# Turned activations moved 4, 8, 16 or 48 bytes inside their tiles, in a one-core kernel of three transformer blocks

## The chip, the cores and the metric

The kernel runs on one core of one Trainium2 chip. The metric is the device time of one execution, in microseconds (us), as the median of several runs; lower is better. One execution was also profiled, and the rows below come from it.

## What is computed

The reference runs three layers on 256 tokens of width 1024, batch 1, everything in float32. The parts that matter here are the large products, activation times weight:

```python
for i in range(DEPTH):                      # two layers
    ...
    h = h + jnp.concatenate([mix, mem_out], axis=-1) @ w_out
    z = rms_norm(h, norm_ffn[i])
    if i % 2 == 0:
        h = h + swiglu(z, ffn_w_gate[j], ffn_w_up[j], ffn_w_down[j])      # width 2816
    else:
        h = h + moe_swiglu(z, moe_router[j], moe_w_gate[j], moe_w_up[j], moe_w_down[j])
...
# third layer (second_block): two kinds of attention, then
f = jnp.square(jax.nn.relu(h @ w_ff1[layer])) @ w_ff2[layer]              # width 4096
```

`moe_swiglu` sends each token to 2 of 8 experts, each a SwiGLU network of inner width 3584. Its weights are 352 MB of the roughly 500 MB that the kernel reads.

## The kernel before

**The products.** Every large product is made of three TensorE passes, so that float32 accuracy is kept with a faster operand type (`float32r`). An activation x is split into a high part and a low part, and so is a weight w; `mm3` (L393) adds xh·wh, xl·wh and xh·wl into one PSUM bank. The first operand of `PE.matmul` is the stationary one: a block of the activation, 128 rows by 128 tokens, that is loaded into the array (LDWEIGHTS in the profile, row PEld). The second operand, the weight, streams past it, mostly 512 columns at a time (MATMUL, row PE). Each of the three passes loads its own stationary block, so there is one load per matmul. `gemm_col` (L398) does products with a weight's columns, `gemm_row` (L428) those of the down projections, both through `mm3` at L394 to L396.

**Turned activations.** The stationary block needs the contraction along the partitions, so activations are turned: TensorE transposes them (L387), and `split` (L374) writes the high part with ScalarE (L375) and the low part with VectorE (L376). The tiles that hold them are
- `xth`, `xtl`: 8 chunks of 256 tokens, made by `new_xt` (L491) for the inputs of the dense products: the attention and convolution projections, both feed-forward networks, the output projections;
- `hth`, `htl` in `ffn` (L919): 4 chunks of 256 tokens, the inner activations of the two dense feed-forward networks;
- `xeh`, `xel` in `gather` (L1446): 8 chunks of 128 tokens, the tokens that one expert was given (L375 and L376 again write them, behind a product with a one-hot matrix at L1453);
- `hth`, `htl` in the expert loop (L1577): 4 chunks of 128 tokens, the inner activations of an expert.

In one place the roles are exchanged: in the convolution's input projection (L1156 to L1158) the weight is stationary and `xth` or `xtl` streams, 256 columns at a time.

**Where the tiles lie.** A partition of SBUF is a row of bytes. The pools are so padded that, in the built program, the left-hand pools begin at multiples of 128 bytes and those on the right-hand side 64 bytes behind one. All the four kinds of turned tile lie at a multiple of 128 bytes, but for the three `new_xt(1)` pairs on the right (the input of the first feed-forward network, `z0`, and the two layers' memory tokens), which lie 64 behind. The chunks inside a tile are 512 or 1024 bytes apart, so each 128-token block begins where its tile does, as far as the place within 128 bytes goes. The weights' high and low parts (`whi`, `wlo`) sit in rings of slots: the five main pairs of slots at multiples of 128, and extra pairs on the right-hand side, used in the mixers and the third layer, 64 behind.

**The weight stream.** `Stream` (L52 on) loads 1 MB pieces of weights in the order of use (SP queue, L93) into a ring of raw slots, ScalarE copies a unit of 128x1024 to its high part (L107), VectorE subtracts to get the low part (L122), and TensorE uses both. A raw slot is loaded again once L122 has read it, a `whi`/`wlo` slot is filled again once TensorE has used it.

**The expert loop** runs over 8 experts and 7 blocks of 512 inner columns each, 56 blocks. One block is 24 passes for the gate, 24 for the up product (stationary `xeh`, `xel`) and 24 for the down product of the block before (stationary `hth`, `htl`), 72 passes of 512 columns in all.

Of the kernel before, what the change touches and what calls it, by code (L numbers as in the profile page):

```python
# [11 lines left out]
F32R = mybir.dt.float32r  # L12
# [11 lines left out]
T = 256  # L24
# [139 lines left out]
def two_blocks(tc, A, out):  # L164
# [14 lines left out]
    def bank(i, shape=(128, 512)):  # L179
        return psp.tile(list(shape), F32, name=f"b{i}", tag=f"b{i}", bufs=1)  # L180
# [26 lines left out]
    def ffn_blocks(width):  # L207
        b = blocks(width)
        return b[-1:] + b[:-1] if b[-1][1] < 512 else b
# [46 lines left out]
    def pool(es, name, bufs, side=None):  # L256
        return es.enter_context(tc.tile_pool(name=name, bufs=bufs, side=side, reuse_waits="tile"))
# [116 lines left out]
    def split(src, hi_, lo_):  # L374
        S.activation(hi_, src, AF.Copy)  # L375
        V.tensor_tensor(lo_, src, hi_.bitcast(F32), op=OP.subtract)  # L376

    def turn(*a):
        run(turns(*a))
# [18 lines left out]
    def gemm_col(o, xt, n, tbs=(0, 1), outer=False):  # L398

        th, tl = xt  # L400
        nu = 8 // (4 if n == 256 else 2)
        na = 8 // nu

        def one(u, i, tb):
            wh, wl = u
            for kk in range(na):
                k = i * na + kk
                mm3(o[tb], th[:, k, tb * 128:tb * 128 + 128], tl[:, k, tb * 128:tb * 128 + 128],
                    wh[:, kk, :], wl[:, kk, :], k == 0, k == 7)

        if outer:
            us = W.take(nu)
            for tb in tbs:
                for i, u in enumerate(us):
                    one(u, i, tb)
                    if tb == tbs[-1]:
                        W.done(1)
                    yield
        else:
            for i in range(nu):  # L420
                u = W.take(1)[0]
                for tb in tbs:
                    one(u, i, tb)
                    if tb == tbs[-1]:
                        W.done(1)
                    yield
# [38 lines left out]
    def run(g):  # L465
        for _ in g:
            pass

    class Bg:
# [12 lines left out]
        def finish(self):  # L482
            while self.g is not None:
                self.pump()
# [3 lines left out]
    xq = ExitStack()  # L488
    xtp = [pool(lv, "xtp", 1), pool(xq, "xtq", 1, "right")]

    def new_xt(i=0):  # L491
        return (xtp[i].tile([128, 8, T], F32R, name="xth"), xtp[i].tile([128, 8, T], F32R, name="xtl"))

    def norm_only(src, grow, xn=None, upd=None, dve=False):
        if xn is None:
# [409 lines left out]
    def ffn(xt, width, gated, t1, finish, tick=lambda: None, free=lambda b: None, near_end=lambda: None):  # L905


        with ExitStack() as es:
            fp = pool(es, "ffn", 2)
            acc = [[bank(4), bank(5)], [bank(6), bank(7)]]  # L910
            prev = None
            rot = 0
            bl = ffn_blocks(width)

            def ticked(g):
                for _ in g:
                    tick()

            def turned(hn, n, rot):  # L919
                ht = (fp.tile([128, 4, T], F32R, name="hth"), fp.tile([128, 4, T], F32R, name="htl"))  # L920
                for tb in range(2):
                    turn(hn[tb], n // 128, ht[0], ht[1], 0, tb, [rot + tb])
                return ht

            late = None
            for fi, (c0, n) in enumerate(bl):
                gv = [bank(rot)[:, 0:n], bank(rot + 1)[:, 0:n]]
                r2 = (rot + 2) % 4
                ub = 6 if fi == 0 else r2
                uv = [bank(ub)[:, 0:n], bank(ub + 1)[:, 0:n]]  # L930
                g = gemm_col(gv, xt, n, outer=fi == 0)
                ug = gemm_col(uv, xt, n, outer=fi == 0) if gated else ()
                if fi == 0:

                    first = [x for x in (g, ug) if x for i in range(8 // (4 if n == 256 else 2))]
                    for i, x in enumerate(first):
                        if i == len(first) - (1 if gated else 1):
                            t1()
                        next(x)
                    W.hold = False  # L940
                    W.most = 1
                if late is not None:

                    for _ in range(4):
                        next(g)
                        tick()
                    prev = (turned(*late), late[1], True)
                    late = None
                    W.most = 99
                ticked(g)  # L950
                hn = [fp.tile([128, 512], F32, name=f"sg{tb}") for tb in range(2)]
                for tb in range(2):
                    S.activation(hn[tb][:, 0:n], gv[tb], AF.Silu if gated else AF.Relu)
                ticked(ug)
                for tb in range(2):
                    V.tensor_tensor(hn[tb][:, 0:n], (uv if gated else gv)[tb], hn[tb][:, 0:n], op=OP.mult)
                free(rot)
                if prev is not None:
                    ticked(gemm_row(acc, prev[0], list(range(prev[1] // 128)), prev[2], False))
                if fi == 0:  # L960
                    late = (hn, n, rot)
                else:
                    prev = (turned(hn, n, rot), n, False)
                rot = r2
            near_end()
            g = gemm_row(acc, prev[0], list(range(prev[1] // 128)), False, True, outer=True)
            for i in range(prev[1] // 128):
                next(g)
            finish(acc, 0)
            run(g)  # L970
            finish(acc, 1)
# [200 lines left out]
    for c in range(6):  # L1172
# [6 lines left out]
        def tick():  # L1179
            dg.pump(3)  # L1180
            dt.pump(3)
            heads.pump(1)
# [249 lines left out]
    mp = pool(mo, "moe", 2)  # L1432
# [12 lines left out]

    def gather(p):  # L1446

        xe = (mp.tile([128, 8, 128], F32R, name="xeh", bufs=1), mp.tile([128, 8, 128], F32R, name="xel", bufs=1))
        for g in range(2):
            b = bank(6 + g)  # L1450
            for j in range(4):
                for tb in range(2):
                    PE.matmul(b[:, j * 128:j * 128 + 128], zN[:, tb, (g * 4 + j) * 128:(g * 4 + j) * 128 + 128],  # L1453
                              p[:, tb], start=tb == 0, stop=tb == 1)
            split(b.rearrange("p (j t) -> p j t", t=128), xe[0][:, g * 4:g * 4 + 4],
                  xe[1][:, g * 4:g * 4 + 4])
        return xe
# [88 lines left out]
    for e in range(NE):  # L1546
        xe = xes.pop(e)
        for fi, (c0, n) in enumerate(bl):
            rot = 2 * ((e * len(bl) + fi) % 2)
            gb, ub = bank(rot), bank(rot + 1)  # L1550
            run(gemm_col([gb], xe, n, tbs=(0,)))
            sg = growp.tile([128, D], F32, name="grow")[:, 0:512]
            S.activation(sg, gb, AF.Silu)
            if last is not None:
                combine(*last, 1)
                last = None
            run(gemm_col([ub], xe, n, tbs=(0,)))
            V.tensor_tensor(sg, ub, sg, op=OP.mult)
            if fi == len(bl) - 1 and e + 1 < NE:
                xes[e + 1] = gather(hot[e + 1])  # L1560
            if prev is not None:
                pe_, pacc, pht, pfi = prev
                run(gemm_row([pacc], pht, list(range(4)), pfi == 0, pfi == len(bl) - 1, tbs=(0,)))
                if pfi == len(bl) - 1:
                    last = (pe_, rows_of(pacc), scatter(hot.pop(pe_)))
            if e == 0 and fi == 1:
                gates()
                mci = counts()
                gcol = const.tile([128, 16], F32, name="gcol")
                for i, nm in enumerate(("mixg", "ffng")):  # L1570
                    V.scalar_tensor_tensor(gcol[:, 8 * i:8 * i + 8], colsA[:, 8 + 24 * i:16 + 24 * i], 1.0,
                                           P[:, R[nm]:R[nm] + 8], op0=OP.add, op1=OP.mult)
            if fi == 4 and e + 1 < NE:
                hot[e + 1] = chosen(e + 1, 0)
            if fi == 0:
                acc = [bank(4), bank(5)]
            ht = tuple(mp.tile([128, 4, 128], F32R, name=f"ht{x}", bufs=1) for x in "hl")  # L1577
            turn(sg, 4, ht[0], ht[1], 0, 0, [rot])
            prev = (e, acc, ht, fi)
            if last is not None:  # L1580
                combine(*last, 0)
# [161 lines left out]
    for g in range(2):  # L1743
        Z, A1 = [], []
        for i in range(4):
# [8 lines left out]
            t = sp_.tile([128, 384], F32, name="ab")  # L1754
# [255 lines left out]
```

## Time and profile before

| what | value |
|---|---|
| median of 3 runs | 1871.54 us (1871.01 to 1878.94) |
| the profiled execution | 1873.42 us |
| its span, first to last instruction | 1871.0 us |
| TensorE busy | 1822.2 us, 97% of the span |
| VectorE busy | 1455.6 us, 78% |
| ScalarE busy | 1227.1 us, 66% |
| weight loads (PEld) busy | 1497.7 us, 80% |
| mean rate of the DMA | 269 GB/s |

The page divides the span in 40 slices; TensorE is at nine tenths or more in all but three of them. A matmul's duration in the profile contains the time in which its last columns run through the array, and successive matmuls overlap. What a pass really costs is the distance from its start to the start of the next one, which is called its pitch below.

### The profile page before, as it was taken

Reading aid. Unit: us, or ns where it says so; the run is one execution under the profiler, and the core shown is the slowest. Engines: PE = TensorE matmul, PEld = TensorE weight load, DVE = VectorE, ACT = ScalarE, POOL = GpSimd, SP = SyncE. Lnnn points to the kernel's source line nnn. Section 1 sums busy time; section 2 is a strip of 40 time slices with the busy share of each in tenths; the row PEclk is TensorE's granted clock in tenths of the full one; section 3 lists DMA queues with packets and bytes.
Section 4 is the critical chain, followed back from the end, with each engine's and each line's share of the span. In section 5 each row is a group of like instructions: output and inputs, shape, how many; then the busy total and the mean of one; then the engine's idle time right before and its main releaser. Section 6 shows DMA issues by size and latency. Waiting matters only on the chain. (4 is left out here: it accounts for less than half of the span.)

```text
span 1871.0 us, 23916 instructions
## 1 busy us (share of the span) xinstructions
PE 1822.2 (97%) x8782; PEld 1497.7 (80%) x8782; DVE 1455.6 (78%) x1743; ACT 1227.1 (66%) x1605; POOL 39.3 (2%) x63
## 2 busy tenths in 40 slices
PE   7999999999999999999999999999999989999998
PEld 6787888898778888788788888887888867678886
DVE  5556988688799899898998998888988864467553
ACT  5645444465588777787787787877877775546442
POOL 1100000000000000000000000000000010010000
PEclk9999999999999999999999999999999999999999
DMA  7325997562699999899999998999999644237540
GB/s 275 134 80 193 397 334 287 196 190 75 230 338 378 341 342 383 321 369 347 343 374 350 338 375 316 366 355 339 368 357 335 248 144 151 75 104 265 183 158 23
DMA packets 224933, 503.95 MB, mean 269 GB/s; under 512 B 8308, under 2 KB 25896, under 8 KB 224808
## 3 DMA queue, kind: packets, MB, share of 16 engines
q1 hardware_dynamic: 223688, 499.37, 74.4%
q0 software_dynamic: 832, 2.46, 0.5%
q8 instruction: 70, 1.15, 0.2%
q10 hardware_dynamic: 288, 0.52, 0.1%
q14 instruction: 55, 0.45, 0.1%
HBM read 501.26 MB, written 1.06 MB: 268 GB/s over the span
## 5 line engine op out<-in xcount | busy, mean ns | idle before, releaser
L122 DVE TENSOR_TENSOR wlo<-wraw,whi 128x1024 fp32r<-128x1024 f32 (+1 forms) x894 | 1053.2, 1219 | 182.5 <-ACT whi L107 171.6
L107 ACT ACTIVATE whi<-wraw 128x1024 fp32r<-128x1024 f32 (+1 forms) x894 | 928.4, 1057 | 265.1 <-PE b L395 238.3
L394 PE MATMUL b<-whi,xeh 128*128 128x512 f32 x896 | 359.2, 401 | 0.0
L396 PE MATMUL b<-wlo,xeh 128*128 128x512 f32 x896 | 349.8, 390 | 0.0
L395 PE MATMUL b<-whi,xel 128*128 128x512 f32 x896 | 349.0, 389 | 0.0
L394 PE MATMUL b<-whi,xth 128*128 128x512 f32 (+2 forms) x656 | 257.1, 392 | 6.3 <-ACT xth L375 2.3
L394 PE MATMUL b<-whi,hth 128*128 128x512 f32 x664 | 261.9, 394 | 0.8 <-PEq L1503 0.6
L395 PE MATMUL b<-whi,htl 128*128 128x512 f32 x664 | 260.9, 393 | 0.4 <-DVE htl L376 0.2
L396 PE MATMUL b<-wlo,hth 128*128 128x512 f32 x664 | 260.7, 393 | 0.0
L395 PE MATMUL b<-whi,xtl 128*128 128x512 f32 (+2 forms) x656 | 251.6, 384 | 1.7 <-DVE xtl L376 0.9
L396 PE MATMUL b<-wlo,xth 128*128 128x512 f32 (+2 forms) x656 | 251.7, 384 | 1.2 <-DVE wlo L122 1.2
L395 PEld LDWEIGHTS b<-whi,xel 128*128 128x128 f32 x896 | 168.4, 188 | 37.0 <-issue 3.3
L394 PEld LDWEIGHTS b<-whi,xeh 128*128 128x128 f32 x896 | 168.3, 188 | 36.3 <-issue 3.3
L396 PEld LDWEIGHTS b<-wlo,xeh 128*128 128x128 f32 x896 | 168.1, 188 | 36.0
L394 PEld LDWEIGHTS b<-whi,xth 128*128 128x128 f32 x656 | 125.3, 191 | 33.0 <-ACT xth L375 4.2
L394 PEld LDWEIGHTS b<-whi,hth 128*128 128x128 f32 x664 | 125.8, 189 | 27.8 <-ACT hth L375 1.3
L395 PEld LDWEIGHTS b<-whi,htl 128*128 128x128 f32 x664 | 125.7, 189 | 27.4 <-DVE htl L376 1.0
L396 PEld LDWEIGHTS b<-wlo,hth 128*128 128x128 f32 x664 | 125.7, 189 | 26.9
L396 PEld LDWEIGHTS b<-wlo,xth 128*128 128x128 f32 x656 | 125.1, 191 | 26.2 <-DVE wlo L122 2.5
L395 PEld LDWEIGHTS b<-whi,xtl 128*128 128x128 f32 x656 | 125.3, 191 | 25.8 <-DVE xtl L376 2.7
L375 ACT ACTIVATE hth<-b 128x512 fp32r<-128x512 f32 (+1 forms) x84 | 48.3, 593 | 87.5 <-PE b L387 87.5
L376 DVE TENSOR_TENSOR htl<-b,hth 128x512 fp32r<-128x512 f32 (+1 forms) x84 | 56.2, 683 | 48.7 <-ACT hth L375 48.7
(348 smaller groups left out, 1438.4 us busy)
## 6 DMA issues: line engine op xcount, KB each, us to landing
wraw<-in_moe_w_gate_dram SPq DMA_DIRECT2D x112, 1024.0 KB
wraw<-in_moe_w_up_dram SPq DMA_DIRECT2D x112, 1024.0 KB
wraw<-in_moe_w_down_dram SPq DMA_DIRECT2D x112, 1024.0 KB
wraw<-in_w_ff_dram SPq DMA_DIRECT2D x32, 1024.0 KB
adw<-in_ada_w_dram SPq DMA_DIRECT2D x24, 1024.0 KB
wraw<-in_w_in_dram SPq DMA_DIRECT2D x12, 1024.0 KB
wraw<-in_ffn_w_gate_dram SPq DMA_DIRECT2D x11, 1024.0 KB
wraw<-in_ffn_w_up_dram SPq DMA_DIRECT2D x11, 1024.0 KB
```

The lines of the kernel that those rows point to most:

```text
L107: nc.scalar.activation(h, r, AF.Copy)
L122: self.nc.vector.tensor_tensor(l, r, h.bitcast(F32), op=OP.subtract)
L375: S.activation(hi_, src, AF.Copy)
L376: V.tensor_tensor(lo_, src, hi_.bitcast(F32), op=OP.subtract)
L394: PE.matmul(o, xh, wh, start=first, stop=False)
L395: PE.matmul(o, xl, wh, start=False, stop=False)
L396: PE.matmul(o, xh, wl, start=False, stop=last)
```

## The change

A helper makes each tile 32 elements (128 bytes) wider and hands out a view that begins `by` elements (of 4 bytes) behind the tile's start:

```diff
+    def shifted(pool_, a, n, name, by, bufs=None):
+
+        kw = {} if bufs is None else {"bufs": bufs}
+        t = pool_.tile([128, a * n + 32], F32R, name=name, **kw)
+        return t[:, by:by + a * n].rearrange("p (a n) -> p a n", n=n)
+
     def new_xt(i=0):
-        return (xtp[i].tile([128, 8, T], F32R, name="xth"), xtp[i].tile([128, 8, T], F32R, name="xtl"))
+        return (shifted(xtp[i], 8, T, "xth", 2), shifted(xtp[i], 8, T, "xtl", 2))
...
             def turned(hn, n, rot):
-                ht = (fp.tile([128, 4, T], F32R, name="hth"), fp.tile([128, 4, T], F32R, name="htl"))
+                ht = tuple(shifted(fp, 4, T, f"ht{x}", 1) for x in "hl")
...
     def gather(p):
 
-        xe = (mp.tile([128, 8, 128], F32R, name="xeh", bufs=1), mp.tile([128, 8, 128], F32R, name="xel", bufs=1))
+        xe = tuple(shifted(mp, 8, 128, f"xe{x}", 4, 1) for x in "hl")
...
-            ht = tuple(mp.tile([128, 4, 128], F32R, name=f"ht{x}", bufs=1) for x in "hl")
+            ht = tuple(shifted(mp, 4, 128, f"ht{x}", 12, 1) for x in "hl")
```

So `xth`/`xtl` begin 8 bytes further (and 72 behind a multiple of 128 for the pairs on the right), the dense `hth`/`htl` 4 bytes, `xeh`/`xel` 16 bytes, and the experts' `hth`/`htl` 48 bytes. Whatever lies behind a widened tile moves by whole multiples of 128 bytes, so that no other tile changes its place within 128 bytes. The instructions of every engine stand in the same order as before, with the same shapes. One wait of the SP queue falls away, that of one load of `conv_w_in` on TensorE.

Counted in the program, the passes by the place of the stationary block (before, and now) are:

| stationary tile | moving columns | passes | before | now |
|---|---|---|---|---|
| `xeh`, `xel` | 512 | 2688 | 0 | 16 |
| experts' `hth`, `htl` | 512 | 1344 | 0 | 48 |
| dense `hth`, `htl` | 512 | 648 | 0 | 4 |
| `xth`, `xtl`, left | 512 | 1152 | 0 | 8 |
| `xth`, `xtl`, right | 512 | 576 | 64 | 72 |
| `xth`, `xtl` | 256 or 268 | 240 | 0, and 96 of them 64 | 8, and 96 of them 72 |
| weight (here `xth`, `xtl` move) | 256 | 288 | `xth` at 0 | `xth` at 8 |

## Rows read from the trace of the kernel before

**Rows 1.** The page's head: span, then busy time, share and instructions by engine.

```profile
span 1871.0 us, 23916 instructions
...
PE 1822.2 (97%) x8782; PEld 1497.7 (80%) x8782; DVE 1455.6 (78%) x1743; ACT 1227.1 (66%) x1605; POOL 39.3 (2%) x63
```

**Rows 2.** Groups of TensorE by line and shape: busy us, mean ns | idle before.

```profile
L394 PE MATMUL b<-whi,xeh 128*128 128x512 f32 x896 | 359.2, 401 | 0.0
...
L394 PE MATMUL b<-whi,hth 128*128 128x512 f32 x664 | 261.9, 394 | 0.8 <-PEq L1503 0.6 <-ACT hth L375 0.2
...
L394 PE MATMUL b<-whi,xth 128*128 128x512 f32 x576 | 232.7, 404 | 3.8 <-ACT xth L1606 1.9 <-ACT xth L375 1.6 <-ACT whi L107 0.3
...
L1156 PE MATMUL b<-xth,whi 128*128 128x256 f32 x96 | 28.1, 292 | 0.2 <-ACT xth L375 0.2
```

**Rows 3.** The expert loop: PE, PEld, DVE, ACT, POOL busy us (count), clock, DMA share, GB/s.

```profile
540.00:1440.00 900.00, 897.86 (x4119) 736.29 (x4118) 802.76 (x773) 697.29 (x742) 0.00 (x0) 1.00 0.97 352
```

**Rows 4.** The longest wait in the expert loop, 700 to 1300 us: total, times, longest us.

```profile
ACT whi L107 <- PE b L395: 72.1, 200, 1.8
```

**Rows 5.** Timeline of TensorE in the expert loop, first and last of 63 passes: start us, us.

```profile
578.72 0.39 PE L394 MATMUL b<-whi,xeh 128*128 128x512 f32 x1
...
592.78 0.39 PE L396 MATMUL b<-wlo,hth 128*128 128x512 f32 x1
```

**Rows 6.** A stretch at the lower granted clock, same columns.

```profile
227.80:231.10 3.30, 3.30 (x10) 2.52 (x9) 2.74 (x4) 0.00 (x0) 0.00 (x0) 0.50 1.05 409
```

**Rows 7.** Timeline of TensorE inside that stretch, first and last of 6 passes.

```profile
228.48 0.63 PE L396 MATMUL b<-wlo,hth 128*128 128x512 f32 x1
...
230.61 0.63 PE L395 MATMUL b<-whi,htl 128*128 128x512 f32 x1
```

**Rows 8.** Timeline of TensorE, first feed-forward network, first and last of 92 passes.

```profile
203.24 0.39 PE L395 MATMUL b<-whi,xtl 128*128 128x512 f32 x1
...
224.06 0.39 PE L396 MATMUL b<-wlo,xth 128*128 128x512 f32 x1
```

**Rows 9.** Timeline of TensorE, convolution's input projection, first and last of 94 passes.

```profile
398.44 0.28 PE L396 MATMUL b<-wlo,xth 128*128 128x256 f32 x1
...
409.60 0.28 PE L1158 MATMUL b<-xth,wlo 128*128 128x256 f32 x1
```

**Rows 10.** Timeline of TensorE, first product of a 256-column block, first and last of 35 passes.

```profile
160.32 0.28 PE L395 MATMUL b<-whi,xtl 128*128 128x256 f32 x1
...
164.18 0.28 PE L396 MATMUL b<-wlo,xth 128*128 128x256 f32 x1
```

**Rows 11.** Timeline of TensorE, the same block's second product, first and last of 47 passes.

```profile
168.01 0.28 PE L395 MATMUL b<-whi,xtl 128*128 128x256 f32 x1
...
173.43 0.28 PE L396 MATMUL b<-wlo,xth 128*128 128x256 f32 x1
```

**Rows 12.** Timeline of TensorE, last feed-forward network, first and last of 49 passes.

```profile
1786.96 0.39 PE L394 MATMUL b<-whi,xth 128*128 128x512 f32 x1
...
1798.16 0.39 PE L394 MATMUL b<-whi,hth 128*128 128x512 f32 x1
```

**Rows 13.** Groups of the splits and of like operations: busy us, mean ns | idle before.

```profile
L376 DVE TENSOR_TENSOR htl<-b,hth 128x512 fp32r<-128x512 f32 x82 | 55.5, 690 | 47.6 <-ACT hth L375 47.6
L375 ACT ACTIVATE hth<-b 128x512 fp32r<-128x512 f32 x82 | 47.7, 598 | 85.4 <-PE b L387 85.4
...
L526 ACT ACTIVATE ka<-b 64x512 f32<-64x512 f32 x8 | 4.5, 588 | 5.7 <-PE b L525 5.6
...
L1910 DVE TENSOR_TENSOR sq<-b,grow 128x512 f32<-128x512 f32 x8 | 5.5, 685 | 4.4 <-PE b L396 4.4
```

**Rows 14.** Waits of the SP queue, whole span: the one that falls away.

```profile
SPq L93 <- PE b L1119: 6.0, 1, 6.0
```

**Rows 15.** The stretch of rows 8, by engine, columns as in rows 3.

```profile
202.22:224.06 21.84, 21.84 (x98) 17.93 (x97) 21.53 (x27) 11.61 (x14) 0.00 (x0) 1.00 1.03 387
```

## The prediction
> **What bounds the kernel now.** I read the page's head first: TensorE is busy 1822.2 us of a span of 1871.0 us [rows 1]. The expert loop shows how tight that is: in 900 us TensorE is busy 897.9 us, VectorE 802.8 us, ScalarE 697.3 us, and the DMA moves 352 GB/s [rows 3]. The longest wait there is ScalarE's, for TensorE to give a weight slot back, 72.1 us in 600 [rows 4]: the others wait for TensorE, not it for them. So the time is the number of passes times their pitch, and a change of pitch shows in the time one for one until VectorE or the DMA runs out. The groups give the numbers: 896 passes of L394 on `xeh`, 664 on `hth`, 576 on `xth` with 512 columns [rows 2]; L395 and L396 have as many each, so 3 x 2136 = 6,408 passes of 512 columns, and 528 shorter ones (the 240 and the 288 of the table of the change).
>
> The pitch is the number to look at. In the expert loop 62 pitches take from 578.72 to 592.78 us, 226.8 ns each [rows 5]. At the full clock of 2.4 GHz 512 columns need 213.3 ns, so 13.5 ns are extra. At the lower clock, granted at 0.50 (1.2 GHz) [rows 6], five pitches take 2.13 us, 426 ns [rows 7], which is 512/1.2: no extra. With 256 columns at full speed 93 pitches take 11.16 us, 120.0 ns [rows 9], against 106.7: an extra of 13.3 ns again. So the extra does not grow with the columns, there is one per pass, and it goes away when the stream is half as fast. It looks like a price that the running pass pays for the load of the next stationary block beside it. That block is what the change moves, so the question is what this extra does.
>
> **What the rows say about place.** Three stretches have another place within 128 bytes. In the first feed-forward network the stationary `z0` lies at 64: 91 pitches in 20.82 us, 228.8 ns [rows 8], 2.0 more than at 0. In the 256-column block of the same network, also at 64, one product has 34 pitches in 3.86 us, 113.5 ns [rows 10], and the other 46 in 5.42 us, 117.8 ns [rows 11], 6.5 and 2.2 less than at 0. In the last network the weights that stream lie at 64 and the stationary block at 0: 48 pitches in 11.20 us, 233.3 ns [rows 12], 6.5 more. So the place does matter, but a step of 64 bytes of the stationary block moved the pitch up in one shape, down in the other, and two products of one shape and place differ by 4.3 ns.
>
> The Trainium skill, TensorE: Matmul & The Clock Gate, Step-by-step, says that the array has two independent read ports and that loading the next tile takes no read bandwidth from the running matmul. By that rule the move costs and gives nothing at all, 0 us in the sum; rows 5 and 8 disagree with it, since the pitch differs by 2.0 ns with the place of the stationary block.
>
> **The change, part by part.**
> - *Stationary blocks, 512 columns.* No row shows one 4, 8, 16 or 48 bytes off. Bounds: from below the whole extra goes, 13.5 ns x 6,408 = 86.5 us gained; from above each pays what a moved stream pays, 6.5 ns x 6,408 = 41.7 us lost. The nearest row is rows 8, the same operand moved by more, +2.0 ns, 12.8 us over 6,408. I take 0: the moves are smaller than 64 bytes, rows 10 and 11 have the other sign, and four different moves on four kinds of tile will average out part of whatever they do.
> - *Stationary blocks, 256 and 268 columns.* 240 passes, between -6.5 and +6.5 ns, so 1.6 us either way. I take 0.
> - *Turned tile as the stream* (L1156 to L1158). 288 passes of 120.0 ns move from 0 to 8. Rows 12 bound it above, 6.5 x 288 = 1.9 us; nothing excludes a gain, of at most 13.3 x 288 = 3.8 us. I take 0.
> - *The writes.* ScalarE's split takes 598 ns and VectorE's 690 [rows 13]. Like operations that write 32 bytes behind a multiple of 128 (`ka` and `sq`) take 588 and 685 [rows 13], so a place off 128 costs nothing there; 4 and 8 bytes are not shown. If such a write took twice as long, an expert block would need 0.7 us more of VectorE, which is idle 97 of 900 us [rows 3], or 1.8 us in a block of 72 passes (16.3 us), so it stays covered. Where that cover is missing, in the first feed-forward network (VectorE 21.53 of 21.84 us [rows 15]), its 12 splits would cost 8.3 us at the worst. A gain has no reason. I take 0.
> - *The wait that falls away.* One load of a convolution weight waited 6.0 us for TensorE on SP's queue [rows 14]. Nothing waited for that load, so earlier is worth nothing; if the load did hold TensorE it would be 6.0 us at most.
> - *The wider tiles* cost no time: order and waits are the same otherwise, and no other tile changes its place within 128 bytes.
>
> The sum is 0 against the profiled execution's 1873.4 us, a span of 1871.0 and 2.4 us around it. The median of the runs lies 1.9 us lower, so I forecast 1871 us.
>
> The Trainium skill, SBUF — State Buffer, Specifications, gives cachelines of 16 bytes and says that each cross to a new line pays. This rule speaks against the moves by 4 and 8 bytes, which spread the 512 bytes of a block over 33 lines where 32 did. As an estimate from that page's line size, one thirty-second of the extra of 13.5 ns is 0.42 ns, on 2,616 passes 1.1 us more, and the sum would be 1872 us; 16 and 48 bytes would cost nothing by it. No row here shows such a line.
>
> **The rivals.**
> - *Faster: the two reads no longer meet.* If the extra comes from stream and load meeting because both begin at 0, a move of a few bytes takes them apart. For it: the extra is always there at 0 and 0, and rows 10 show that 6.5 ns of it can go by place alone. Against it: at 64 the 512-column pitch rose. All passes freed would be 1785 us; if the experts' 4,032 passes (or about as many of several kinds) lose half of the extra, 6.7 x 4,032 = 27 us, the time is 1844 us. VectorE would allow that in the expert loop (10.8% idle [rows 3]) and so would the DMA, which moves 387 GB/s elsewhere [rows 15]; in the first feed-forward network VectorE is full and nothing would be gained.
> - *Slower: an off place makes the load collide longer.* Blocks that begin off 128 touch five pieces of 128 bytes and not four. At the price of rows 8 on all passes the time is 1871 + 13 = 1884 us, at the price of rows 12 it is 1913. It decides from 1.5 ns per pass, where 6,408 passes make 9.4 us. For it: both 512-column stretches off 0 are slower. Against it: rows 10 and 11.
> - *The change does not do what it says:* on the right-hand side the tile goes from 64 to 72, not to 8. Those 576 passes keep 228.8 ns or pay up to 233.3, at most 2.6 us, inside the forecast.
>
> **How the numbers follow.** About 0.5%, 9.4 us, is what a measurement here can tell from no change. No change within that has 0.38, since the nearest rows disagree in sign and the moves differ by kind. Faster has 0.34: the extra is 6% of every pass, a large thing to hit. Slower has 0.28, as the 512-column rows off 0 point that way. The range reaches down to 1838 us, past the 1844 of the faster rival, and up to 1893, past the 1884 of the slower one; beyond it lie a large release of the extra (about 0.11) and a price like that of rows 12 (about 0.08). The forecast's own range is 1862 to 1880 us.
>
> **What would show it.** In the changed profile: the pitch on TensorE's timeline in the expert loop, one for the passes on `xeh` and `xel` and one for those on `hth` and `htl`, and in each dense network. If I am right they stay within 1.5 ns of 226.8 on average; if one kind falls to 220 or less, the first rival holds for it; if they go to 229 or 233, the second does. The splits should stay at 598 and 690 ns. A new idle time of TensorE before L394 to L396 would show a cover that was lost. The forecast is wrong if the kinds move together in one direction.

## The result and the profile after

The changed kernel takes 1890.66 us (median of 5 runs, 1888.85 to 1895.02) against 1872.27 us for the kernel before (5 runs, 1871.01 to 1878.94): a ratio of 1.0089, 95% interval 1.0068 to 1.0109. It is slower by 0.9%, 18 us. Comparisons here and below leave disturbed runs out.

The page's head, the expert loop, the longest wait there and the splits of the changed kernel, in the order of [rows 1], [rows 3], [rows 4] and [rows 13], each from the view named there:

```profile
span 1888.9 us, 23915 instructions
...
PE 1840.8 (97%) x8782; PEld 1501.5 (79%) x8782; DVE 1462.2 (77%) x1743; ACT 1227.2 (65%) x1605; POOL 39.3 (2%) x63
```

```profile
540.00:1440.00 900.00, 897.86 (x4058) 727.59 (x4057) 796.76 (x763) 685.99 (x731) 0.00 (x0) 1.00 0.95 347
```

```profile
ACT whi L107 <- PE b L395: 72.0, 189, 1.8
```

```profile
L376 DVE TENSOR_TENSOR htl<-b,hth 128x512 fp32r<-128x512 f32 x82 | 55.5, 691 | 49.4 <-ACT hth L375 49.4
L375 ACT ACTIVATE hth<-b 128x512 fp32r<-128x512 f32 x82 | 47.8, 599 | 86.8 <-PE b L387 86.8
```

The span grew by 17.9 us and TensorE's busy time by 18.6 us, so nothing new is waited for. In the same 900 us TensorE is as busy as before, at the same granted clock of 1.00, but has 4,058 matmuls where it had 4,119. The wait for weight slots is what it was, and the splits take 599 and 691 ns where they took 598 and 690. The whole loss is in the pitch.

The pitch is read from TensorE's timeline. First two stretches of the expert loop with 47 passes each, expert 0 and expert 1 (first and last pass of each), and the same stretches by engine:

```profile
564.42 0.40 PE L395 MATMUL b<-whi,xel 128*128 128x512 f32 x1
...
575.25 0.39 PE L396 MATMUL b<-wlo,xeh 128*128 128x512 f32 x1
...
692.58 0.39 PE L395 MATMUL b<-whi,xel 128*128 128x512 f32 x1
...
703.01 0.40 PE L396 MATMUL b<-wlo,xeh 128*128 128x512 f32 x1
```

```profile
564.42:575.25 10.83, 10.83 (x47) 8.70 (x46) 9.55 (x10) 9.19 (x10) 0.00 (x0) 1.00 1.00 350
692.58:703.01 10.43, 10.43 (x47) 8.64 (x46) 8.99 (x10) 9.20 (x10) 0.00 (x0) 1.00 0.99 361
```

Expert 0 needs 10.83 us for 46 pitches, 235.4 ns; expert 1 needs 10.43 us, 226.7 ns, as in [rows 5]. The two have their `xeh` and `xel` in the same place, the same clock and nearly the same DMA load. Nor does the pitch belong to the expert. Within expert 2, whose `xeh` and `xel` are written once, 47 passes of its first block and 47 of its fourth are:

```profile
763.66 0.39 PE L395 MATMUL b<-whi,xel 128*128 128x512 f32 x1
...
774.10 0.40 PE L396 MATMUL b<-wlo,xeh 128*128 128x512 f32 x1
...
819.09 0.40 PE L395 MATMUL b<-whi,xel 128*128 128x512 f32 x1
...
829.82 0.40 PE L396 MATMUL b<-wlo,xeh 128*128 128x512 f32 x1
```

These are 10.44/46 = 227.0 and 10.73/46 = 233.3 ns. In the whole loop the passes on `xeh` and `xel` take about 226.8 ns in the third to seventh block of every odd expert and in the first block of the even one behind it; in the third to seventh block of every even expert, and in the first of the odd one behind it, they take 233 to 235.7. The change from one to the other comes in an expert's second block, in which TensorE also runs four passes of L1485 for the expert before; what in it does this, no run shows.

Then, on the same timeline, the experts' `hth`/`htl` (24 passes), the dense `hth`/`htl` (47), `z0` (95) and the last network with its weights from the right-hand slots (47):

```profile
703.24 0.40 PE L394 MATMUL b<-whi,hth 128*128 128x512 f32 x1
...
708.55 0.39 PE L396 MATMUL b<-wlo,hth 128*128 128x512 f32 x1
```

```profile
267.62 0.40 PE L395 MATMUL b<-whi,htl 128*128 128x512 f32 x1
...
278.32 0.39 PE L396 MATMUL b<-wlo,hth 128*128 128x512 f32 x1
```

```profile
204.46 0.40 PE L395 MATMUL b<-whi,xtl 128*128 128x512 f32 x1
...
226.20 0.39 PE L396 MATMUL b<-wlo,xth 128*128 128x512 f32 x1
```

```profile
1775.88 0.39 PE L395 MATMUL b<-whi,xtl 128*128 128x512 f32 x1
...
1786.61 0.39 PE L396 MATMUL b<-wlo,xth 128*128 128x512 f32 x1
```

The four are 5.31/23 = 230.9, 10.70/46 = 232.6, 21.74/94 = 231.3 and 10.73/46 = 233.3 ns. The last is what [rows 12] gave; `z0` has gone from 228.8 [rows 8] to 231.3. Means over all consecutive passes of a kind (distances under 245 ns) give the loss kind by kind:

| passes of 512 columns | number | before, ns | after, ns | us |
|---|---|---|---|---|
| `xeh`, `xel` | 2688 | 227.7 | 231.2 | +9.5 |
| experts' `hth`, `htl` | 1344 | 226.9 | 230.6 | +5.0 |
| dense `hth`, `htl`, main weight slots | 432 | 226.9 | 230.2 | +1.5 |
| `xth`, `xtl` left, main weight slots | 852 | 228.9 | 231.3 | +2.1 |
| `xth`, `xtl` right | 576 | 229.1 | 231.2 | +1.2 |
| all with right-hand weight slots | 516 | 233.3 | 233.0 | -0.2 |

The sum is 19.1 us for a span that grew by 17.9: the pitch accounts for all of it.

### The profile page after: what moved, and what is told of

Read it like the earlier page. It is cut to its first block, busy times and chain, and to the rows that moved or that the text cites. A ratio compares the mean times of both kernels' runs of the same rounds, so it can differ in the third digit from the quotient of the medians.

```text
span 1888.9 us, 23915 instructions
## 1 busy us (share of the span) xinstructions
PE 1840.8 (97%) x8782; PEld 1501.5 (79%) x8782; DVE 1462.2 (77%) x1743; ACT 1227.2 (65%) x1605; POOL 39.3 (2%) x63
## 5 line engine op out<-in xcount | busy, mean ns | idle before, releaser
L394 PE MATMUL b<-whi,xeh 128*128 128x512 f32 x896 | 363.6, 406 | 0.0
L396 PE MATMUL b<-wlo,xeh 128*128 128x512 f32 x896 | 352.5, 393 | 0.0
L394 PE MATMUL b<-whi,hth 128*128 128x512 f32 x664 | 263.4, 397 | 1.1 <-PEq L1509 0.9
L394 PE MATMUL b<-whi,xth 128*128 128x512 f32 (+2 forms) x656 | 258.0, 393 | 5.7 <-ACT xth L1612 1.9
L396 PE MATMUL b<-wlo,hth 128*128 128x512 f32 x664 | 262.4, 395 | 0.0
L396 PE MATMUL b<-wlo,xth 128*128 128x512 f32 (+2 forms) x656 | 251.9, 384 | 1.4 <-DVE wlo L122 1.4
L394 PEld LDWEIGHTS b<-whi,xeh 128*128 128x128 f32 x896 | 168.4, 188 | 38.7 <-issue 3.4
L396 PEld LDWEIGHTS b<-wlo,xeh 128*128 128x128 f32 x896 | 168.2, 188 | 38.7
L394 PEld LDWEIGHTS b<-whi,xth 128*128 128x128 f32 x656 | 124.9, 190 | 32.7 <-ACT xth L375 3.3
L394 PEld LDWEIGHTS b<-whi,hth 128*128 128x128 f32 x664 | 126.2, 190 | 29.5 <-ACT ptok L1471 1.1
L396 PEld LDWEIGHTS b<-wlo,hth 128*128 128x128 f32 x664 | 125.2, 189 | 28.6
L396 PEld LDWEIGHTS b<-wlo,xth 128*128 128x128 f32 x656 | 124.4, 190 | 27.8 <-DVE wlo L122 2.7
```

The source lines that it names most:

```text
L394: PE.matmul(o, xh, wh, start=first, stop=False)
L396: PE.matmul(o, xh, wl, start=False, stop=last)
```

## The experiments

Twelve kernels ran, in three groups, each beside runs of the kernel before on its own chip (medians 1875.68, 1874.6 and 1873.65 us). Pitches without a row are means over the consecutive passes of one place in the trace of that run. Where an edit adds lines, L394 to L396 have a larger number.

### One place for all, and a map of places

In the first group the tiles keep the change's extra 128 bytes. One kernel begins every view exactly there, 128 bytes in:

```diff
-        return (shifted(xtp[i], 8, T, "xth", 2), shifted(xtp[i], 8, T, "xtl", 2))
+        return (shifted(xtp[i], 8, T, "xth", 32), shifted(xtp[i], 8, T, "xtl", 32))
...
-                ht = tuple(shifted(fp, 4, T, f"ht{x}", 1) for x in "hl")
+                ht = tuple(shifted(fp, 4, T, f"ht{x}", 32) for x in "hl")
...
-        xe = tuple(shifted(mp, 8, 128, f"xe{x}", 4, 1) for x in "hl")
+        xe = tuple(shifted(mp, 8, 128, f"xe{x}", 32, 1) for x in "hl")
...
-            ht = tuple(shifted(mp, 4, 128, f"ht{x}", 12, 1) for x in "hl")
+            ht = tuple(shifted(mp, 4, 128, f"ht{x}", 32, 1) for x in "hl")
```

> All four kinds of turned tile begin 128 bytes into their widened tiles, so they stay displaced and 128 bytes wider, but lie at the place within 128 bytes that they had before. If the place within 128 bytes is what costs (my theory), the pitch of 512-column passes in the expert loop goes back to 226.7 ns and the time to that of the kernel before, 1872 us within 0.3%. If the wider tiles, or the changed distance between a high and a low tile, cost it (rival), the pitch stays near 231 ns and the time near 1890 us.

Measured: 1899.01 us, ratio 1.0104 (1.0034 to 1.0174). Its timeline in the expert loop, 47 passes on `xeh`, `xel`:

```profile
1004.80 0.40 PE L395 MATMUL b<-whi,xel 128*128 128x512 f32 x1
...
1015.53 0.39 PE L396 MATMUL b<-wlo,xeh 128*128 128x512 f32 x1
```

10.73/46 = 233.3 ns, at a place that is a multiple of 128 like that of before. The place within 128 bytes, on which the prediction had argued, is not what counts.

A second kernel gave each expert and each block another place inside the 128 bytes, a third and a fourth moved the five main pairs of weight slots too, by 64 and by 32 bytes:

```diff
+XE_BY = (0, 1, 2, 4, 8, 12, 16, 24)
+HT_BY = (0, 4, 12, 1, 16, 8, 24)
...
+        xe = tuple(shifted(mp, 8, 128, f"xe{x}", XE_BY[min(turned_for[0], 7)], 1) for x in "hl")
...
+            ht = tuple(shifted(mp, 4, 128, f"ht{x}", HT_BY[fi], 1) for x in "hl")
```

> Only the experts' tiles are moved: the stationary gate and up blocks by 0, 4, 8, 16, 32, 48, 64, 96 bytes for experts 0 to 7, the down blocks by 0, 16, 48, 4, 64, 32, 96 bytes for the seven blocks of each expert; weights stay at 0. If any place off a multiple of 128 costs about the same (theory A), every place but 0 reads 229 to 234 ns in place of 226.7. If the cost is one of lines crossed (rival: more 16-byte lines for 4 and 8, none for 16, 32, 48, 64, 96), only 4 and 8 read more than 226.7. If the place matters by where the stream and the load meet (theory B), the places differ from each other by several ns and some may read under 226.7. The time has no meaning of its own here; about 1880 us by theory A.

> As the run before, but all main weight slots, the operand that streams, begin 64 bytes behind a multiple of 128. If each operand has to begin at a multiple of 128 by itself (theory A), every place of the stationary block reads 233 ns or more, 64 too. If the distance between the two counts (theory B), the expert whose blocks lie at 64 reads 226.7 again and the one at 0 reads 233.3, which is what the last network showed on the right-hand side. Time by theory A 1910 us, by theory B a little less.

> As the run before with the weight slots 32 bytes behind a multiple of 128. Theory A: all places 229 to 234 ns. Theory B: the expert whose blocks lie at 32 reads 226.7, and the pitches of the other places are those of the map with weights at 0, moved by 32 bytes. Should any pair read under 226.7 ns, it is a candidate for a faster kernel.

Measured: 1896.63, 1898.33 and 1895.45 us, one run each. As maps of the place they failed: nearly every kind ran at 230 to 234 ns, also those that begin where their tile does (231.2 ns for expert 0 of the first of them, moved by 0). Something that all three share had spoilt nearly every place, and the only thing that they share with the change is the tile's width.

### The two halves of the change

A widened `xeh` puts its low partner `xel` 128 bytes further, and with it the tiles behind. So the width was tried alone, and the move alone with tiles 512 bytes wider:

```diff
-        xe = tuple(shifted(mp, 8, 128, f"xe{x}", 4, 1) for x in "hl")
+        xe = tuple(shifted(mp, 8, 128, f"xe{x}", 0, 1) for x in "hl")
```

(and 0 for the other three kinds), and

```diff
-        t = pool_.tile([128, a * n + 32], F32R, name=name, **kw)
+        t = pool_.tile([128, a * n + 128], F32R, name=name, **kw)
```

> Half of the change: all four kinds of tile 128 bytes wider, but no view moved inside. New theory after the first runs (C): what counts is the place within 512 bytes, the length of a stationary block; before, streams and blocks nearly all lay at one place within 512, and the 128 bytes of width push every low tile, and the tiles behind it, off that place by 128 or more. By C the time is that of the change, 1885 to 1900 us, and the expert loop reads 230 ns and more. Rival (A, the place within 128 bytes): nothing has moved, 1872 us and 226.7 ns.

> The other half: the views moved by 8, 4, 16 and 48 bytes as in the change, but the tiles 512 bytes wider in place of 128, so that high and low tiles and everything behind them keep their place within 512 bytes. If the small moves cost by themselves, the expert loop reads 229 to 236 ns and the time is 1880 to 1900 us. If only the width did it, 226.7 ns and 1872 us. By C I expect a cost in between, since stationary blocks lie 8 to 48 bytes off the stream's place but high and low ones alike: 1880 us.

Measured: the width alone 1892.45 us, ratio 1.0102 (1.0079 to 1.0125); the move alone 1887.44 us, ratio 1.0065 (1.0042 to 1.0089). The timeline of the first, 47 passes on `xeh`, `xel` and 95 on `z0`:

```profile
1057.41 0.40 PE L395 MATMUL b<-whi,xel 128*128 128x512 f32 x1
...
1068.04 0.39 PE L396 MATMUL b<-wlo,xeh 128*128 128x512 f32 x1
```

```profile
204.78 0.40 PE L395 MATMUL b<-whi,xtl 128*128 128x512 f32 x1
...
226.72 0.40 PE L396 MATMUL b<-wlo,xth 128*128 128x512 f32 x1
```

231.1 and 233.4 ns, though no view is moved inside its tile. Split by what is loaded, the pitch is 227.3 ns where two `xeh` blocks (which stayed) follow each other, and 233.1 where one of the two is `xel` (128 bytes off). The timeline of the second, 47 passes on `xeh`, `xel` (moved by 16) and 24 on the experts' `hth`, `htl` (moved by 48):

```profile
1054.96 0.39 PE L395 MATMUL b<-whi,xel 128*128 128x512 f32 x1
...
1065.39 0.40 PE L396 MATMUL b<-wlo,xeh 128*128 128x512 f32 x1
```

```profile
702.72 0.40 PE L394 MATMUL b<-whi,hth 128*128 128x512 f32 x1
...
708.09 0.39 PE L396 MATMUL b<-wlo,hth 128*128 128x512 f32 x1
```

226.7 and 233.5 ns: 16 bytes cost nothing in this stretch, 48 bytes 6.7 ns. Over the whole loop the passes moved by 16 have a mean of 227.6 ns, against 227.7 before, though a part of every expert's second block held 233.2. Either half makes a loss, and the two don't add (1.02 + 0.65% against 0.89%): a pass that is off its place mostly costs 230 to 235 ns, whichever half put it there.

### The map, with the low tiles in place

With tiles 512 bytes wider the high and the low part lie alike, and the tables of places work:

```diff
+XE_BY = (0, 16, 32, 48, 64, 80, 96, 112)
+HT_BY = (0, 1, 2, 4, 8, 12, 24)
```

then `XE_BY = (1, 2, 4, 8, 12, 24, 124, 120)` with `HT_BY = (0, 32, 64, 96, 112, 80, 48)`, and in the last group `XE_BY = (36, 40, 44, 52, 54, 58, 62, 63)` with `HT_BY = (0, 5, 6, 20, 28, 56, 61)`, in elements of 4 bytes.

> Tiles 512 bytes wider; the experts' gate and up blocks moved by 0, 64, 128, 192, 256, 320, 384, 448 bytes for experts 0 to 7, high and low alike, the down blocks by 0, 4, 8, 16, 32, 48, 96 bytes for the seven blocks of each expert, all else at the old place within 512. By C expert 0 and the dense networks read 226.7 ns, the other experts differ by place, and 448 and 64 differ most from 256. By A experts 0, 2, 4 and 6 all read 226.7. A place under 226.7 would be worth a kernel of its own.

> As the run before: gate and up blocks moved by 4, 8, 16, 32, 48, 96 bytes for experts 0 to 5, and by 16 and 32 bytes to the other side (496 and 480) for experts 6 and 7; down blocks by 0, 128, 256, 384, 448, 320, 192 bytes. By C moves of 4 to 16 bytes change the pitch by less than 2 ns, those of 96 by 3 to 7 ns, and the two sides differ. By A all read 229 to 236 ns and only the down blocks at 0, 128, 256 and 384 read 226.7.

> The rest of the map of distances in one run, tiles 512 bytes wider: xeh and xel by expert at 144, 160, 176, 208, 216, 232, 248 and 252 bytes behind a multiple of 256, the experts' hth and htl by block at 0, 20, 24, 80, 112, 224 and 244. Theory A: all but 0 are slower than 226.7 ns, between 227.6 (measured at 240) and 234.1 (measured at 96); 224 gives 233.2 as before; the whole kernel about 1890 us. Rival E (somewhere in the map the load and the stream no longer meet): a place under 226 ns, which would be a version to build.

Measured: 1890.36, 1891.54 and 1898.2 us, one run each. The timeline of the first, 47 passes on `xeh`, `xel` at 256, 320, 384 and 448 bytes:

```profile
1052.23 0.39 PE L397 MATMUL b<-whi,xel 128*128 128x512 f32 x1
...
1062.70 0.40 PE L398 MATMUL b<-wlo,xeh 128*128 128x512 f32 x1
...
1178.99 0.39 PE L397 MATMUL b<-whi,xel 128*128 128x512 f32 x1
...
1189.73 0.39 PE L398 MATMUL b<-wlo,xeh 128*128 128x512 f32 x1
...
1324.26 0.39 PE L397 MATMUL b<-whi,xel 128*128 128x512 f32 x1
...
1334.94 0.40 PE L398 MATMUL b<-wlo,xeh 128*128 128x512 f32 x1
...
1434.83 0.40 PE L397 MATMUL b<-whi,xel 128*128 128x512 f32 x1
...
1445.37 0.39 PE L398 MATMUL b<-wlo,xeh 128*128 128x512 f32 x1
```

227.6, 233.5, 232.2 and 229.1 ns. The means over all passes of these four experts are 227.6, 233.3, 232.6 and 229.3 ns; those of the experts at 0, 64, 128 and 192 are 227.3, 233.3, 232.6 and 229.3. The curve repeats every 256 bytes. With this and the 4 bytes of the next map, at 232.4 ns, theory C of the forecasts, a place within 512 bytes, falls. And the nearest place below, 252 bytes, in the timeline of the last map:

```profile
1439.89 0.39 PE L397 MATMUL b<-whi,xel 128*128 128x512 f32 x1
...
1450.63 0.40 PE L398 MATMUL b<-wlo,xeh 128*128 128x512 f32 x1
```

233.5 ns, four bytes from the best place. All the points of the three maps, means over the passes of one place, as the distance from the streaming weight to the next stationary block, modulo 256 bytes:

| distance | pitch, ns | distance | pitch, ns | distance | pitch, ns |
|---|---|---|---|---|---|
| 0 | 226.7 to 227.7 | 64 | 233.4 | 192 | 229.1 |
| 4 | 232.4 | 80 | 232.0 | 208 | 232.5 |
| 8 | 230.7 | 96 | 234.0 | 216 | 232.1 |
| 16 | 227.6 to 230.0 | 112 | 233.3 | 224 | 233.3 |
| 20 | 233.2 | 128 | 232.6 | 232 | 231.5 |
| 24 | 230.6 | 144 | 233.4 | 240 | 227.6 |
| 32 | 233.3 | 160 | 233.3 | 244 | 232.4 |
| 48 | 233.3 | 176 | 230.0 | 248, 252 | 233.2, 233.4 |

No place is below the best one of the kernel before. Some of these means mix two levels: at 16 the down blocks of the first map run at 226.7 ns in four experts and at 233.3 in the other four, and at 244 they run at 226.7 in one expert and at 233.0 to 233.5 in the other seven.

### Distance, or place?

But for the two kernels that moved the weights and failed as maps, the main weight slots had lain at 256 behind a multiple of 512 up to here, so that a distance and a place could not be told apart but by the right-hand side. One kernel moves blocks and main weight slots together by 96 bytes, one moves every view by 256:

```diff
+    hlA.tile([128, 24], F32, name="padm")
+    after_hl = top.enter_context(tc.tile_pool(name="afterhl", bufs=1))
+    after_hl.tile([128, 8], F32, name="padn")
...
-        t = pool_.tile([128, a * n + 32], F32R, name=name, **kw)
+        t = pool_.tile([128, a * n + 64], F32R, name=name, **kw)
...
-        xe = tuple(shifted(mp, 8, 128, f"xe{x}", 4, 1) for x in "hl")
+        xe = tuple(shifted(mp, 8, 128, f"xe{x}", 56, 1) for x in "hl")
```

(the other three kinds by 56 too; the pads themselves move what lies behind by 128), and, with tiles 512 bytes wider,

```diff
-        xe = tuple(shifted(mp, 8, 128, f"xe{x}", 4, 1) for x in "hl")
+        xe = tuple(shifted(mp, 8, 128, f"xe{x}", 64, 1) for x in "hl")
```

> The changed kernel with all left-hand turned tiles and the five main pairs of weight slots at 96 behind a multiple of 256 bytes: nothing on the left begins at a multiple of 128, and the distance from stream to block is 0. Theory A (distance modulo 256): 226.8 ns in the expert loop on all passes; the whole kernel about 1875 us, since z0 (distance 64, 576 passes at 233.3 for 229.1 ns, 2.4 us) and the weights from the right-hand slots (distance 160, not yet measured, 516 passes) stay off. Rival C (a stationary block that begins off 128 or 256 bytes is slow by itself): 232 ns or more in the expert loop, 1895 us or more, as where the block lay at 96 and the weight at 0 (234.1 ns).

> The changed kernel with every view begun 256 bytes behind its tile's start and the tiles 512 bytes wider. Theory A (distance modulo 256): nothing is lost, 226.8 ns in the expert loop and 1872 us, ratio 1.000. Rival D (any view that does not begin at its tile, or a wider tile, costs): 1880 us or more.

Measured: 1873.84 us, ratio 0.9998 (0.9981 to 1.0015), and 1872.20 us, ratio 0.9995 (0.9983 to 1.0008). The timelines, 47 passes on `xeh`, `xel` of the one and of the other:

```profile
1044.78 0.39 PE L398 MATMUL b<-whi,xel 128*128 128x512 f32 x1
...
1055.23 0.39 PE L399 MATMUL b<-wlo,xeh 128*128 128x512 f32 x1
```

```profile
1045.05 0.40 PE L395 MATMUL b<-whi,xel 128*128 128x512 f32 x1
...
1055.51 0.39 PE L396 MATMUL b<-wlo,xeh 128*128 128x512 f32 x1
```

227.2 and 227.4 ns. At 96 bytes with the weights at 0 a block ran at 234.0, at 96 with the weights at 96 it runs at 227.2: the distance decides, not the place. In the first kernel `z0` now has a distance of 64 and runs at 233.3 ns where it ran at 229.1, as the table says. A moved view is harmless when it is moved by 256.

### A kernel that beats both

If distance 0 is the best, the kernel before leaves something: its right-hand pools lie 192 bytes off the left-hand ones. One pad puts them right:

```diff
-    ends.tile([128, 8], F32, name="pade")
+    ends.tile([128, 56], F32, name="pade")
```

> The kernel before, with a pad on the right-hand side that is 192 bytes larger, so that the right-hand pairs of turned tiles and the right-hand weight slots lie 256 behind a multiple of 512 bytes, like the left-hand ones. Theory A (the pitch goes by the distance from the streaming weight to the next stationary block, modulo 256 bytes, and is least at 0): the 576 passes on z0 go from 229.1 to 226.8 ns, 1.3 us; the 516 passes with weights from the right-hand slots from 233.3 to 226.8 ns, 3.4 us; the 256-column passes of the first network lose up to 0.4 us. In all 4 us less than before, 1868 us against 1872 (ratio 0.998). Rival B (these passes are slower because of what else runs in those networks, VectorE and the DMA at their limits): the pitches and the time stay, ratio 1.000.

Measured: 1870.02 us (12 runs) against 1873.65 (29 runs), ratio 0.9974 (0.9959 to 0.9990), 4.9 us less by the ratio. The timeline, the stretches of [rows 8] (`z0`, 95 passes) and of [rows 12] (last network, 47 passes):

```profile
205.43 0.40 PE L395 MATMUL b<-whi,xtl 128*128 128x512 f32 x1
...
226.75 0.39 PE L396 MATMUL b<-wlo,xth 128*128 128x512 f32 x1
...
1760.98 0.40 PE L395 MATMUL b<-whi,xtl 128*128 128x512 f32 x1
...
1771.41 0.39 PE L396 MATMUL b<-wlo,xth 128*128 128x512 f32 x1
```

226.8 and 226.7 ns, from 228.8 and 233.3. What VectorE and the DMA do in these networks did not hold the passes. The profiled execution was the slowest of the twelve (1873.54 us, mean granted clock 0.987 where that of before had 0.990), so the gain is read from the runs, and only the pitch from the profile.

## Why the prediction was wrong

The forecast of 1871 us, no change, was wrong; the time lies in the range, 2 us from its upper end, on the side of the slower rival. The prediction's own sign of being wrong came: all kinds but those with right-hand weight slots moved together, up by 2.1 to 3.7 ns.

- *What bounds the kernel* was right: TensorE's passes times their pitch, and a change of pitch showed one for one.
- *"Stationary blocks, 512 columns"* is the step that failed. It was taken as 0 between -86.5 and +41.7 us; with the wider tiles it measured +19.1. The reasons given for 0 were that the moves are smaller than 64 bytes, that rows 10 and 11 have the other sign, and that four moves average out. But 4 bytes cost 5.7 ns and 48 cost 6.7, so the size of the move says little; rows 10 and 11 have 256 columns, where distance 0 is the slower place, which says nothing of 512 columns; and as no distance is better than 0, there was nothing to average against. Had I read the rows by distance, [rows 8] (192 bytes) and [rows 12] (64 bytes) were two points of one curve, both above [rows 5] (0), and the term a loss.
- *"The wider tiles cost no time, no other tile changes its place within 128 bytes"* failed too: the low tiles moved by 128 modulo 256, and that alone cost 1.0%.
- *The other steps held.* The 256- and 268-column passes and the streaming `xth` changed by half a microsecond at most, the splits by 1 ns, and the wait that falls away showed no gain; it wasn't tried by itself.
- *The faster rival* falls for 512 columns: no point of the map is below 226.7 ns, so none frees any of the extra 13.5 ns.
- *The slower rival* had the right sign, and 1884 us at the price of [rows 8] is 7 us short. Its mechanism, blocks that touch five pieces of 128 bytes, falls: at 96 and 96, and moved by 16, blocks touch five pieces and run at 227.2 and 226.7 ns.
- *The third rival* (the right-hand tiles go to 72) cost 1.2 us, within its bound of 2.6; with the rule of distance they went from 192 to 200 and, their low partners, to 72.

The Trainium skill, TensorE: Matmul & The Clock Gate, Step-by-step, has the load of the next tile take no read bandwidth from the running matmul; the runs here disagree, as the pitch of the same passes goes from 226.7 to 234.0 ns by nothing but the distance between what is loaded and what streams. The Trainium skill, SBUF — State Buffer, Specifications, with its lines of 16 bytes would have 16 and 48 bytes cost nothing and 4 bytes 0.4 ns, by the prediction's estimate from that line size; measured are 0 to 3 ns on average, 6.7 ns and 5.7 ns.

What stays open is why distance matters, and why the same passes on the same stationary tiles hold 226.8 ns in some blocks of the changed kernel and 233 to 235.7 in others. There `xeh` lies at distance 16 and `xel` at 144, where the map, in which both parts lie alike, has 233.4 ns, and yet 226.8 holds in 23 of the 56 blocks. So distance is shown as a cause of the loss, by moving it away and back, but the table gives no pitch for each single pass. The passes of a stretch repeat a cycle of three (240, 232 and 235 ns for expert 0), so each seems to hand its lag to the next, but that is argued, not shown.

## What to carry to other kernels

Where every pass loads a stationary block while the one before it streams, count the addresses of the two, both parts of a split operand included, modulo 256 bytes: here equal places were the best of 25 that were measured, and the others cost up to 7.3 ns of each pass, 3%. A tile made wider by 128 bytes moves its neighbours, so a helper that pads should pad by a multiple of 256, and two pools that feed the same products should begin alike; the count needs one list of addresses and no run. Whether the rule holds for other types and lengths is not shown: the passes of 256 columns here go the other way.

## What the runs showed that was not expected

- Four bytes are enough: distance 0 gives 226.7 to 227.7 ns, 4 gives 232.4, 252 gives 233.4, while 16 and 240 can stay near 227.6.
- The curve has a period of 256 bytes: 0 and 256, 64 and 320, 128 and 384, 192 and 448 agree within 0.3 ns.
- For 256 columns another curve holds: at distance 192 the kernel before had 113.5 and 117.8 ns [rows 10, 11]. In the kernel that beats both, the same passes, now at distance 0, took 119.6 and 119.9 ns on average, 4 ns more, 0.4 us over 96. The 120.0 ns of [rows 9], half of whose passes have the weight as the stationary block, are about the same.
- One place can have several pitches: 226.7, 233.3 and 235.4 ns on the same `xeh` and `xel`, by block of the loop, at the same granted clock of 1.00 and nearly the same DMA load.
